# Values of a chunked delta rule: turned in 32x32 blocks by VectorE and placed by four stores, with their row factors moved into the inverse

## The chip, the cores and the metric

The kernel runs on one core of a Trainium2 chip. The metric is the device time of one execution in microseconds (us); the kernel before takes 1234.93 us, the median of three runs (1234.6 to 1235.82).

## The reference

One decoder layer in float32: 1024 tokens, 1024 channels. A shared RMS-norm and input projection feed two groups of heads, differential attention (4 heads) and a gated DeltaNet (4 heads, key and value width 128); both outputs go through one output projection, and a squared-ReLU MLP follows. The change lies in the DeltaNet's delta rule. Cut to what matters:

```python
dn_qkv = causal_conv_silu(dn_qkv, conv_w[l])            # width 4, depthwise
dn_q, dn_k, dn_v = jnp.split(dn_qkv, ...)
dn_q, dn_k = l2_norm(dn_q), l2_norm(dn_k)               # per head of 128
# chunked: k_beta = k * beta, v_beta = v * beta
Lmat = where(strict, einsum('bhncd,bhnjd->bhncj', k_beta, k) * decay, 0)
sol = triangular_solve(Lmat, [v_beta, k_beta * exp(g)], unit_diagonal=True)
u, w = sol[..., :Dv], sol[..., Dv:]
def step(state, inp):                                   # one chunk after the other
    v_new = u_c - w_c @ state
    o = (q_c * exp(g_c)) @ state + qk_c @ v_new
    state = state * exp(g_last) + k_dec.T @ v_new
```

## The kernel before

The kernel uses chunks of 128 tokens, eight in all. The DeltaNet part has two stages.

**Projections and inverse.** `dn_proj(kind)` (L666) projects keys (kind 1), then queries (kind 0), then values (kind 2). Each kind has 4 heads `h` in two halves `hf` of 512 tokens, so 8 groups. A group is 24 products on TensorE (PE) into the PSUM tile `ps_dn` (L265 to L267; two banks), with channels on the partitions and tokens along the row; ScalarE (ACT) copies it to `cp` (L678), and ACT and VectorE (DVE) compute the convolution in `cy` (L680, L682) and SiLU (L690). `skew` hands each group on one group late. Every group is then turned by PE so that tokens lie on the partitions: `transposed(src)` (L713) issues four 128x128 transposes into the PSUM tile `ps_t` (L716). What the second stage needs is parked in DRAM by `park` (L701): `park_d[h, chunk, token, slot, channel]`, one store per group and slot, 512 bytes per token. Slot 0 holds the keys, slot 1 the scaled turned keys, slot 2 the values, slot 3 the queries, slot 4 the masked query-key products.

Keys are not normalised; the factors are carried instead. `vsc` (128 x 32, one column for each head and chunk) holds the square root of the keys' sums of squares `ssk` plus epsilon for each token. The values' turned tile in PSUM is multiplied by `vsc` (L854) into the SBUF tile `kn` (two buffers) and parked in slot 2.

The unit-triangular matrix of each head and chunk (`lt`) is inverted by blocks of 32. The 32x32 diagonal blocks go through DRAM (`fsx_d`, `fsg_d`) and are solved in VectorE by `invert` (L743), which is interleaved with the queries' groups. `horner(hs, hf)` (L797) then builds the inverse W of two heads and one half: 4 loads `gb` a head (L804, rows of 128 bytes), a VectorE block turn (L806), a product `ps_p` (L810) masked into `pb` by VectorE (L813), and three rounds of products `ps_h` (L818; 96, 64 and 32 wide) whose results go back into W, the first by VectorE (L822), the others by ACT (L824). It is called after the values' groups with `hf == 0`, four times: heads 0 and 1, heads 2 and 3 of the first half, then of the second.

**Scan.** `scan` (L902) walks the chunks. It loads slots 0 to 2 of a chunk as `pka` (L910), multiplies the keys with the state, and forms

```python
V.scalar_tensor_tensor(rr_[h], PA[h], neg_eg[:, i:i + 1], pk[:, h, 2, :], ALU.mult, ALU.add)
Wc = W[h, c // 4][:, (c % 4) * P:(c % 4 + 1) * P]
T.matmul(PA[h], Wc, rr_[h], start=True, stop=True)      # contracts over W's rows
```

where `neg_eg` is minus the exponential of the summed gates. For the first chunk `rr_` is slot 2 itself. The product over W sums over the partitions, that is over W's rows and the rows of `rr_`.

**Order.** In the first stage a scheduler orders each engine's instructions by its own simulated times. From the scan on, the class `Interleave` plans the order of PE's work by hand: the scan, the attention's projections (`ps_qk`, L1067 to L1069, with their turns `ps_qkt`, L1028), scores and values of the attention. Nearly all DMAs are issued in order from SyncE's queue (SP): parks, `gb`, the weight quarters `wraw` (L191 and L217), `pka`, `pkb`. A DMA on this queue also waits for the one issued eight before it to land, whose semaphore it takes over.

Of the kernel before, what the change touches and what calls it, by code (L numbers as in the profile page):

```python
# [13 lines left out]
ALU = mybir.AluOpType  # L14
# [106 lines left out]
def tile_hymba_layer(  # L121
# [6 lines left out]
    nc = tc.nc  # L128
    V, S, G, T = nc.vector, nc.scalar, nc.gpsimd, nc.tensor
# [40 lines left out]
    park_d = dram.tile([HEADS, NT, P, 5, P], F32, name="park_d")  # L170
# [212 lines left out]
    def z_raw(tb, u, pool, tag, mid=None, at=2):  # L383

        ps = pool.tile([P, 512], F32, tag=tag, name="ps_z")
        for k in range(KB):
            if k == at and mid is not None:
                z_spread(mid)
            T.matmul(ps[:, :UC], xTs[tb][:, k, :], wz[u][1][k // 2][:, k % 2, :], start=k == 0, stop=k == KB - 1)
        return ps  # L390
# [88 lines left out]
    with tc.manual_schedule(engines={T.engine, V.engine, S.engine, G.engine}):  # L479
# [5 lines left out]
        z = {(0, 0): z_raw(0, 0, pj, "pj")}  # L485
# [43 lines left out]
        for tb in range(3, NT):  # L529
            for u in range(2):  # L530
                nxt, at = spread_at.get((tb, u), (None, 0))
                z[tb, u] = z_mm(tb, u, *pools[tb], nxt, at)
                if nxt is not None:
# [4 lines left out]
                    if nxt in (4, 5):  # L538
                        b = {4: 5, 5: 7}[nxt]
# [32 lines left out]
    ps = ph.tile([P, 512], F32, tag="ph", name="ps_pv")  # L572
# [24 lines left out]
    v4 = lambda t: t.rearrange("p (c d) -> p c d", d=P)  # L597
    c32 = lambda name: sp.tile([P, 32], F32, name=name)
    beta, gg, neg_eg, eg, elast, ediff = (c32(n) for n in ("beta", "gg", "neg_eg", "eg", "elast", "ediff"))
# [35 lines left out]
    ps = ph.tile([P, 512], F32, tag="ph", name="ps_g")  # L635
# [21 lines left out]
    def ta(name, bufs, dt=F32):  # L657
        return sa.tile([P, 512], dt, tag=name, name=name, bufs=bufs)

    ssq, ssk, rq, bp, kds, vsc = smalls + [sp.tile([P, 32], F32, name=n) for n in ("kds", "vsc")]  # L660

    cps = [sa.tile([P, 1028], F32, name=f"cp{i}") for i in range(2)]
    for cp in cps:
# [2 lines left out]
    def dn_proj(kind):  # L666
        for pr in range(2):
            with tc.issue_after(x_last.ins) if kind == 1 and pr == 0 else ExitStack():
                w = load_unit(w_units[6 + 2 * kind + pr])
            for hl in range(2):  # L670
                h = 2 * pr + hl
                u = 4 * kind + h
                cp = cps[hl]
                for hf in range(2):
                    ps = pj.tile([P, 512], F32, tag="pj", name="ps_dn")
                    trn(ps, w, hl * P, hf)
                    b = 512 * hf
                    S.copy(cp[:, 3 + b:3 + b + 512], ps)  # L678
                    y = ta("cy", 2)
                    S.activation(y, cp[:, 3 + b:3 + b + 512], AF.Copy, scale=pv[:, 36 + u:37 + u])  # L680
                    for wi in (2, 1, 0):
                        V.scalar_tensor_tensor(y, cp[:, wi + b:wi + b + 512], pv[:, 12 * wi + u:12 * wi + u + 1],  # L682
                                               y, ALU.mult, ALU.add)
                    if kind == 1:
                        th = ta("cth", 2)
                        S.activation(th, y, AF.Tanh, scale=0.5)
                        yield h, hf, y, th
                    else:
                        o = ta("cth" if hf else "k2", 2)
                        S.activation(o, y, AF.Silu)  # L690
                        yield h, hf, o

    def skew(gen):
        prev = None
        for it in gen:
            if prev is not None:
                yield prev
            prev = it
        yield prev

    def park(h, hf, slot, src):  # L701
        nc.sync.dma_start(park_d[h, 4 * hf:4 * hf + 4, :, slot, :].rearrange("c p d -> p c d"), v4(src))

    def cols4(t, h, hf):
        return t[:, 8 * h + 4 * hf:8 * h + 4 * hf + 4]

    def bc_col(t):
        return t.unsqueeze(2).broadcast_to([P, 4, P])

    def bc_mask(t):  # L710
        return t.unsqueeze(1).broadcast_to([P, 4, P])

    def transposed(src):  # L713
        ps = pt_.tile([P, 512], F32, tag="pt", name="ps_t")
        for c in range(4):
            T.transpose(ps[:, c * P:(c + 1) * P], src[:, c * P:(c + 1) * P], ident)  # L716
        return ps
# [25 lines left out]
    def invert():  # L743

        fxv = fx.rearrange("p (j i) -> p j i", i=32)
        fgv = fg.rearrange("p (r c) -> p r c", c=32)
        nc.sync.dma_start(fx, fsx_d)
        for j in range(31):
            m = 31 - j
            tv = ft[:, :m * (j + 1)].rearrange("p (m c) -> p m c", m=m)  # L750
            V.tensor_tensor(tv, fxv[:, j, j + 1:32].unsqueeze(2).broadcast_to([P, m, j + 1]),
                            fgv[:, j, 0:j + 1].unsqueeze(1).broadcast_to([P, m, j + 1]), ALU.mult)
            V.tensor_tensor(fgv[:, j + 1:32, 0:j + 1], fgv[:, j + 1:32, 0:j + 1], tv, ALU.subtract)
            if j % 8 == 7:
                yield
        nc.sync.dma_start(fsg_d, fg)

    lt = {}
    for h, hf, y, th in skew(dn_proj(1)):
# [3 lines left out]
        ps = transposed(k2)  # L763
# [33 lines left out]
    def horner(hs, hf):  # L797
        pb, z = {}, {}
        for h in hs:
            gb = gbs[h]  # L800
            for b in range(4):
                bs = slice(32 * b, 32 * b + 32)
                p0 = 32 * h + 8 * b + 4 * hf
                nc.sync.dma_start(v4(gb[bs, :])[:, :, bs], fsg_d[p0:p0 + 4, :].rearrange("c (r k) -> r c k", k=32))  # L804
            z[h] = sp.tile([P, 512], F32, tag="lw", name="W", bufs=10)
            V.transpose(z[h], gb)  # L806
        for h in hs:
            ps = ph.tile([P, 512], F32, tag="ph", name="ps_p")
            for c in range(4):
                T.matmul(ps[:, c * P:c * P + 96], lt[h, hf][:, c * P:(c + 1) * P],  # L810
                         gbs[h][:, c * P:c * P + 96], start=True, stop=True)
            pb[h] = sf.tile([P, 512], F32, tag="pb", name="pb", bufs=2)
            V.tensor_tensor(v4(pb[h])[:, :, 0:96], v4(ps)[:, :, 0:96], bc_mask(blk)[:, :, 0:96], ALU.mult)  # L813
        for m in (96, 64, 32):
            for h in hs:
                ps = ph.tile([P, 512], F32, tag="ph", name="ps_h")
                for c in range(4):
                    T.matmul(ps[0:m, c * P:c * P + m], pb[h][:, c * P:c * P + m],  # L818
                             z[h][:, (c + 1) * P - m:(c + 1) * P], start=True, stop=True)
                zv, pv4 = v4(z[h])[0:m, :, P - m:P], v4(ps)[0:m, :, 0:m]  # L820
                if m == 96:
                    V.tensor_tensor(zv, zv, pv4, ALU.subtract)  # L822
                else:
                    S.activation(zv, pv4, AF.Copy, scale=-1.0)  # L824
        for h in hs:
            W[h, hf] = z[h]

    inverse = invert()
    for h, hf, q2 in skew(dn_proj(0)):
        k2 = ta("kr", 2)  # L830
        nc.sync.dma_start(v4(k2), park_d[h, 4 * hf:4 * hf + 4, :, 0, :].rearrange("c p d -> p c d"))
        park(h, hf, 3, q2)
        ps = transposed(q2)
        psm = gram(k2, q2)
        sq = ta("kn", 2)
        for c in range(4):
            i = cidx(h, 4 * hf + c)
            S.activation(sq[:, c * P:(c + 1) * P], ps[:, c * P:(c + 1) * P], AF.Square, accum_out=ssq[:, i:i + 1])
        rstd(cols4(rq, h, hf), cols4(ssq, h, hf), float(P), EPS * P, sp, "rqt", 4)
        qk = ta("qk", 2)  # L840
        for c in range(4):
            i = cidx(h, 4 * hf + c)
            cs = slice(c * P, (c + 1) * P)
            V.scalar_tensor_tensor(qk[:, cs], psm[:, cs], bp[:, i:i + 1], dts[h, hf][:, cs], ALU.mult, ALU.mult)
        park(h, hf, 4, qk)
        next(inverse, None)
# [2 lines left out]

    heads = [((h, h + 1), hf) for hf in range(2) for h in (0, 2)]  # L850
    for h, hf, v2 in skew(dn_proj(2)):
        ps = transposed(v2)
        vs = ta("kn", 2)
        V.tensor_tensor(v4(vs), v4(ps), bc_col(cols4(vsc, h, hf)), ALU.mult)  # L854
        park(h, hf, 2, vs)
        if hf == 0:
            horner(*heads.pop(0))

# [1059 lines left out]
```

## Time and profile before

| | |
|---|---|
| runs, median of 3 (us) | 1234.93 (1234.6 to 1235.82) |
| profiled execution (us) | 1234.74 |
| its span, first to last instruction (us) | 1233.0 |
| granted TensorE clock | 1.000 |
| values' projections and inverse, about (us of the span) | 186 to 253 |
| first product of the scan (us of the span) | 256.56 |
| DMA, mean over the span | 164 GB/s |

The page lists the busy time of each engine (PEld is the loading of weights into PE, which overlaps PE), the chain of work that ended last, the costliest groups of instructions, and the DMA issues. PE's matmuls are pipelined and their ends are modelled, so how much PE loses is read from what it waited for and from the chain rather than from its busy share alone. Rows of the chain give start, length and what; rows of instructions give the number, then the shortest, median and longest duration in ns.

### The profile page before, as it was taken

The numbers are of one execution on the slowest core, as the hardware profiler recorded it, in microseconds if no ns is written. First come the engines' busy times: TensorE is split into PE (matmuls) and PEld (weight loads), VectorE is DVE, ScalarE is ACT, GpSimd is POOL, SyncE is SP. The second block draws the span as 40 slices with busy tenths as digits, with TensorE's granted clock in tenths as the row PEclk, the third lists the DMA queues.
The fourth block names the chain that finished last, engine by engine and source line by source line (L and its number), as shares of the span: only waits on it lengthen the run. The fifth ranks groups of instructions, "written<-read, shape, count | busy, mean of one in ns | idle before, by whom it ended". The sixth has DMA issues, their size and how long they took to land.

```text
span 1233.0 us, 18819 instructions
## 1 busy us (share of the span) xinstructions
PE 1217.3 (99%) x6823; PEld 1054.3 (86%) x6823; DVE 824.7 (67%) x1524; ACT 624.2 (51%) x1249; POOL 151.3 (12%) x215
## 2 busy tenths in 40 slices
PE   9999999999999999999999999999999999999998
PEld 8978888898999998888888888888888888888886
DVE  6868796556647657777799544565569755777543
ACT  6588553344346555566666544444564333333330
POOL 2411110043434421001200000000000000000000
PEclk9999999999999999999999999999999999999999
DMA  9344653278748756323437434444479645423301
GB/s 350 98 115 122 163 162 104 63 234 240 231 148 252 232 162 159 85 77 108 157 117 255 172 122 151 171 170 153 155 241 382 234 179 184 163 103 103 137 35 69
DMA packets 143301, 202.12 MB, mean 164 GB/s; under 512 B 20920, under 2 KB 98280, under 8 KB 143208
## 3 DMA queue, kind: packets, MB, share of 16 engines
q1 hardware_dynamic: 138584, 187.28, 46.9%
q0 software_dynamic: 4480, 13.64, 2.9%
q8 instruction: 54, 0.88, 0.3%
q14 instruction: 39, 0.32, 0.1%
q10 hardware_dynamic: 144, 0.00, 0.0%
HBM read 135.86 MB, written 65.01 MB: 163 GB/s over the span
## 4 chain that ended last, share of the span: by engine, by line
PE 88%; DVE 4%; DMA 3%; ACT 2%; issue 2%; POOL 1%; SPq 1%; POOLq 0%; DVEq 0%; ACTq 0%
PE X L1517 4%; PE X L1515 4%; PE X L1516 4%; PE X L1814 4%; PE X L1815 4%; PE X L1813 4%; PE ps_dn L265 3%; PE ps_dn L267 3%; PE ps_dn L266 3%; PE ps_qk L1067 3%; PE ps_qk L1068 3%; PE ps_qk L1069 3%; PE ps_o L1250 2%; PE Y L1515 2%; PE Y L1517 2%; PE Y L1516 2%
## 5 line engine op out<-in xcount | busy, mean ns | idle before, releaser
L1433 ACT CAST hH<-ur 128x1024 fp32r<-128x1024 f32 x56 | 58.9, 1051 | 173.4 <-PE Y L1814 89.8
L1434 DVE TENSOR_TENSOR hL<-ur,hH 128x1024 fp32r<-128x1024 f32 x56 | 68.3, 1223 | 79.4 <-ACT hH L1433 79.4
L1067 PE MATMUL ps_qk<-wH,hH 128*128 128x256 f32 x384 | 114.3, 298 | 0.0
L1069 PE MATMUL ps_qk<-wH,hL 128*128 128x256 f32 x384 | 108.7, 283 | 0.0
L1068 PE MATMUL ps_qk<-wL,hH 128*128 128x256 f32 x384 | 108.4, 282 | 0.0
L1434 DVE TENSOR_TENSOR op<-raw,op 128x1024 fp32r<-128x1024 f32 x48 | 58.7, 1223 | 74.2 <-PE X L1516 41.1
L1813 PE MATMUL X<-hH 128*128 128x512 f32 x224 | 87.1, 389 | 0.0
L1814 PE MATMUL X<-hL,hH 128*128 128x512 f32 x224 | 87.1, 389 | 0.0
L1815 PE MATMUL X<-hH,hL 128*128 128x512 f32 x224 | 87.1, 389 | 0.0
L265 PE MATMUL ps_dn<-hH,wH 128*128 128x512 f32 x192 | 76.3, 397 | 0.2 <-ACT cp L678 0.2
L267 PE MATMUL ps_dn<-hH,wL 128*128 128x512 f32 x192 | 75.8, 396 | 0.0
L266 PE MATMUL ps_dn<-hL,wH 128*128 128x512 f32 x192 | 75.8, 395 | 0.0
L1068 PEld LDWEIGHTS ps_qk<-wL,hH 128*128 128x128 f32 x384 | 73.4, 191 | 0.2
L1067 PEld LDWEIGHTS ps_qk<-wH,hH 128*128 128x128 f32 x384 | 73.3, 191 | 0.2
L1069 PEld LDWEIGHTS ps_qk<-wH,hL 128*128 128x128 f32 x384 | 73.1, 190 | 0.0
L1434 DVE TENSOR_TENSOR hL<-dw,hH 128x1024 fp32r<-128x1024 f32 x56 | 68.2, 1218 | 0.9 <-ACT hH L1433 0.9
L1433 ACT CAST op<-raw 128x1024 fp32r<-128x1024 f32 x48 | 50.4, 1052 | 35.7 <-PE Y L1517 19.9
L1433 ACT CAST hH<-dw 128x1024 fp32r<-128x1024 f32 x56 | 58.7, 1048 | 10.7 <-DMA dw<-in_w_down_dram 5.0
L1205 ACT ACTIVATE pexp<-pexp,mx 128x128 f32<-128x128 f32 (+7 forms) x64 | 49.7, 777 | 25.1 <-DVE mx L1204 24.5
L682 DVE SCALAR_TENSOR_TENSOR cy<-cp,pv,cy 128x512 f32<-128x512 f32 x72 | 53.7, 747 | 8.1 <-ACT cy L680 7.3
L1340 PE MATMUL ps_op<-wH,hH 128*128 128x512 f32 x128 | 53.0, 414 | 0.0
L1515 PE MATMUL Y<-hH,op 128*128 128x512 f32 x128 | 49.9, 390 | 0.4 <-DVE ua L1555 0.4
(370 smaller groups left out, 3429.1 us busy)
## 6 DMA issues: line engine op xcount, KB each, us to landing
ur<-ud SPq DMA_DIRECT2D x28, 1024.0 KB, 5.0
raw<-in_w_up_dram SPq DMA_DIRECT2D x32, 512.0 KB, 3.9
dw<-in_w_down_dram SPq DMA_DIRECT2D x32, 512.0 KB, 6.8
wraw<-in_w_units_dram SPq DMA_DIRECT2D x48, 256.0 KB, 3.7
qk_d<-qa POOLq DMA_DIRECT2D x32, 256.0 KB, 4.3
ud<-ua SPq DMA_DIRECT2D x16, 512.0 KB, 4.2
ud<-s SPq DMA_DIRECT2D x16, 512.0 KB, 2.7
pka<-park_d SPq DMA_DIRECT2D x32, 192.0 KB, 4.8
```

The costliest lines, as they stand in the source:

```text
L265: T.matmul(ps, lh(k), rh(k), start=(k == 0), stop=False)
L266: T.matmul(ps, lh(k), rl(k), start=False, stop=False)
L267: T.matmul(ps, ll(k), rh(k), start=False, stop=(k == n - 1))
L1067: T.matmul(ps[:, :256], hH[:, k, sl], wh[:, k, :], start=(k == 0), stop=False)
L1068: T.matmul(ps[:, :256], hH[:, k, sl], wl[:, k, :], start=False, stop=False)
L1069: T.matmul(ps[:, :256], hL[:, k, sl], wh[:, k, :], start=False, stop=(k == KB - 1))
L1433: S.copy(dst[0], src)
L1434: V.tensor_tensor(dst[1], src, dst[0].bitcast(F32), ALU.subtract)
L1515: T.matmul(ps, op[0][:, k, cs], h[0][:, k, :], start=start and k == 0, stop=False, skip_group_check=True)
L1813: T.matmul(bank[t], v[0][:, j, sl], v[2][:, j], start=s0, stop=False, skip_group_check=True)
L1814: T.matmul(bank[t], v[0][:, j, sl], v[3][:, j], start=False, stop=False, skip_group_check=True)
L1815: T.matmul(bank[t], v[1][:, j, sl], v[2][:, j], start=False, stop=s1, skip_group_check=True)
```

## The change

The values' groups are no longer turned on PE. VectorE's transpose turns each 32x32 block of the 128x512 tile in place, from SBUF to SBUF, so that inside a block tokens lie on the partitions, while the blocks stay where channels were on the partitions. Four stores for each group then put the blocks where they belong in slot 2: store `a` takes the 32 partitions of channel block `a` and writes, for each of its 512 tokens, 32 channels (128 bytes). The values are parked without the factor `vsc`. The factor is multiplied into W instead: after `horner` has finished a head, VectorE multiplies W's rows by `vsc`. Since the other term of `rr_` would then get the factor too, `neg_eg` is divided by `vsc` once, ahead of the queries' groups; the tile for the reciprocals, `rvs`, is that of `ssk`, which is not read any more.

```diff
     ssq, ssk, rq, bp, kds, vsc = smalls + [sp.tile([P, 32], F32, name=n) for n in ("kds", "vsc")]
+    rvs = ssk
...
+    def put_blocks(dst, src):
+
+        for a in range(4):
+            s = slice(32 * a, 32 * a + 32)
+            nc.sync.dma_start(dst[:, s].rearrange("(b s) r -> s b r", s=32),
+                              src[s].rearrange("s (b r) -> s b r", r=32))
...
         for h in hs:
+            V.tensor_tensor(v4(z[h]), v4(z[h]), bc_col(cols4(vsc, h, hf)), ALU.mult)
             W[h, hf] = z[h]
 
+    V.reciprocal(rvs, vsc)
+    V.tensor_tensor(neg_eg, neg_eg, rvs, ALU.mult)
     inverse = invert()
...
     for h, hf, v2 in skew(dn_proj(2)):
-        ps = transposed(v2)
         vs = ta("kn", 2)
-        V.tensor_tensor(v4(vs), v4(ps), bc_col(cols4(vsc, h, hf)), ALU.mult)
-        park(h, hf, 2, vs)
+        V.transpose(vs, v2)
+        put_blocks(park_d[h, 4 * hf:4 * hf + 4, :, 2, :].rearrange("c p d -> (c p) d"), vs)
         if hf == 0:
             horner(*heads.pop(0))
```

## The prediction

> **What bounds the kernel now.** I read the page first, then PE's own waits over the whole span, then the stretches around the change, then the chain through them.
>
> ```profile
> span 1233.0 us, 18819 instructions
> PE 1217.3 (99%) x6823; PEld 1054.3 (86%) x6823; DVE 824.7 (67%) x1524; ACT 624.2 (51%) x1249; POOL 151.3 (12%) x215
> PE 88%; DVE 4%; DMA 3%; ACT 2%; issue 2%; POOL 1%; SPq 1%; POOLq 0%; DVEq 0%; ACTq 0%
> PE ps_qkt L1028 <- DVE qn L1092: 1.3, 2, 1.0
> PE ps_dn L265 <- ACT cp L678: 0.2, 1, 0.2
> ```
>
> PE is busy 99% of the span and carries 88% of the chain; the longest waits it has on another engine in mid-kernel are near 1 us, and in the projections that the change touches (ps_dn) there is one of 0.2 us. So an instruction taken from PE's queue is worth its place there, as long as nothing else becomes late. Next, the stage: up to 186 us the keys and queries are projected, 186 to 231 are the projections of the values with the first two pairs of heads of the inverse, 231 to 257 the rest of the inverse up to the scan's first product (columns: start and end, length, PE, PEld, DVE, ACT, POOL busy, granted clock, DMA share, GB/s).
>
> ```profile
> 130.00:186.00 56.00, 56.00 (x300) 47.61 (x299) 51.04 (x138) 30.43 (x99) 8.16 (x8) 1.00 0.59 164
> 186.00:231.00 45.00, 45.00 (x273) 38.09 (x272) 28.89 (x53) 15.50 (x34) 1.01 (x1) 1.00 0.33 88
> 231.00:240.00 9.00, 9.00 (x93) 8.59 (x92) 4.31 (x7) 4.19 (x10) 0.00 (x0) 1.00 0.30 90
> 240.00:257.00 17.00, 16.40 (x177) 15.42 (x176) 8.76 (x22) 4.72 (x15) 3.81 (x4) 1.00 0.42 132
> ```
>
> PE is full until 240. VectorE is busy 28.89 + 4.31 + 8.76 = 41.96 of 71 us (59%), the DMA engines a third. Only behind 240 does PE stand idle at times: there the small products of the inverse wait for VectorE and ScalarE. The chain through the stage (start, length, what; longest pieces):
>
> ```profile
> 189.29 0.44 PE ps_t L716 x4
> 196.79 0.44 PE ps_t L716 x4
> 200.88 0.44 PE ps_t L716 x4
> 211.34 0.59 PE ps_t L716 x4
> 216.22 0.59 PE ps_t L716 x4
> 220.71 1.76 PE ps_p L810 x16
> 223.88 0.44 PE ps_t L716 x4
> 226.17 1.36 PE ps_h L818 x16
> 231.55 1.08 PE ps_h L818 x16
> 232.63 0.59 PE ps_t L716 x4
> 235.73 0.62 PE ps_h L818 x16
> 236.35 0.32 PE ps_qk L1067
> 238.94 0.88 PE ps_p L810 x8
> 240.94 0.52 DVE pb L813
> 242.07 0.58 DVE kn L854
> 253.26 0.26 PE ps_qkt L1028
> 256.72 0.34 PE ps_A L930 x3
> ```
>
> **The change part by part.** *PE's turns go.* Eight groups of four transposes leave the queue. Seven of them stand in the chain: 4 x 0.44 + 3 x 0.59 = 3.53 us; the eighth, in the idle stretch behind 240, I take at 0.44. Sum 3.97, 4.0 us. The lower bound is 8 x 0.44 = 3.5: the three longer ones follow a ps_h and may hold some of its end, which another product would then pay.
>
> *VectorE.* Eight products from PSUM (L854) go, eight block turns of the same 128x512 come, eight products over W, and two small 128x32 operations. The trace has both kinds:
>
> ```profile
> L854 DVE TENSOR_TENSOR kn<-ps_t,vsc x8: 650/683/692, 190.1 to 242.0; 128x512 f32<-128x512 f32 x8
> L806 DVE STREAM_TRANSPOSE W<-gb x8: 690/702/712, 196.8 to 241.4; 128x512 f32<-128x512 f32 x8
> L822 DVE TENSOR_TENSOR W<-W,ps_h x8: 532/544/551, 205.6 to 251.1; 96x384 f32<-96x384 f32 x8
> ```
>
> The turn costs 0.702 for 0.683, no difference. The product over W does not occur before; its row neighbours are L854 (0.683 for 512 columns) and L822 (0.544 for 384, in proportion 0.73). I take 0.68: 8 x 0.68 = 5.4 us, VectorE at 47.4 of 71 us (67%). In the sum over the stage that is free, PE's work hides it; in VectorE's queue it is not, see the tail. The turn no longer waits for PE, which makes it due earlier, as soon as ScalarE's SiLU has written the values. The scaled neg_eg is made while the queries are projected (the first of the three stretches, where VectorE is 51.04 of 56 us busy) and read in the scan; two operations of 32 columns are under 0.68 each by the rows for 512, and PE is full there all the same: nothing.
>
> *The stores.* Each 256 KB store of 512 runs of 512 B becomes four of 64 KB with 512 runs of 128 B. Thirty-two instead of eight on SP's queue, ahead of the small gb loads of the inverse (L804), the weight loads (L191, L217) and, at the end, the scan's pka loads.
>
> ```profile
> L702 SPq DMA_DIRECT2D park_d<-kn x8: 370/378/642, 190.8 to 242.7; - x8
> DMA to landing us min/median/max: 2.3/2.3/2.3
> 200.63 3.38 SPq L804 DMA_DIRECT2D gb<-fsg_d  x7
> gb<-fsg_d SPq DMA_DIRECT2D x32, 16.0 KB, 1.9
> fsx_d<-lt SPq DMA_DIRECT2D x32, 16.0 KB, 1.7
> q1 hardware_dynamic: 1010, 0.12, 24.1%
> q1 hardware_dynamic: 525, 0.26, 81.6%
> 249.42 3.66 SPq L910 DMA_DIRECT2D pka<-park_d  x8
> pka<-park_d SPq DMA_DIRECT2D x32, 192.0 KB, 4.8
> SPq L702 <- DVE kn L854: 13.1, 5, 8.0
> ```
>
> The two q1 rows are the queue between 196.8 and 200 us (gb loads alone, 128 B runs) and between 226 and 227 (one store alone, 512 B runs): 0.241 x 16 x 3.2 / 1010 = 12 ns of a DMA engine per short run, 0.816 x 16 x 1.0 / 525 = 25 ns per long one. So 32 x 512 = 16384 short runs cost 16384 x 12 ns / 16 = 12.5 us of all engines, where 8 x 512 x 25 / 16 = 6.5 went before: 6 us more in 71 at a share of a third. On SP an issue costs 0.378 whatever the run size, if it goes by the number of runs (512 in both): 24 x 0.378 = 9.1 us more on a queue that stands 13.1 us waiting for kn alone (last row). The other bound is that it goes by short runs as the gb loads do: 3.38 / 7 = 0.48 us for 128 of them, so 1.93 for 512. I take 0.38, since the store row has the very count of runs and only their size differs. Who waits behind the stores: gb (needed for ps_p; in the built order the first ps_p stands 63 projection products behind the last query product where it stood 48 behind, so loads late by 3 x 0.378 = 1.1 us find a later reader), the last two weight quarters L191 (ScalarE's cast waits for them with the next PSUM copies behind it; ps_dn's second bank gives it one group of projections), and pka.
>
> *The tail, where the cover goes.* The built order moves 24 ps_qk products to before the second pair's last ps_h; behind it stand 18 instead of 42, all of them in pair three. PE's work from that ps_h's end (236.35) to the first ps_qkt (253.26): 42 ps_qk at (238.94 - 236.35) / 20 = 0.13, 5.5 us; two pairs at 1.76 + 1.36 + 1.08 + 0.62 = 4.82, 9.6; one ps_t, 0.44. That is 15.5 of 16.9 us, so 1.4 idle. After: 18 x 0.13 + 9.6 = 12.0 and the idle time worked out by VectorE's order. Pair three: its pb products stand behind two products over W (2 x 0.68, from 0.3 us after the last ps_h of pair two), then pb 0.52, turn 0.70, pb 0.52: the second pb ends 3.4 us in, PE has had 1.76 + 0.68 = 2.4 us of work: 0.9 idle. Pair four: W, half as wide a qn product, W (0.68 + 0.34 + 0.68) ahead of pb, 0.5 idle against ps_p. The hops from ps_h over VectorE or ScalarE to the next ps_h cost the idle 1.4 of before in four of them, 0.35 each; three stand uncovered now, 1.05. Sum 2.4, 1.0 more than before, although the kn product of 0.58 leaves that chain; bounds 1.4 (nothing more) and twice the 2.4. The first pb of pair four also gates pka (it holds the memory that the scan's tiles take): it issues at 249.42, 7.3 us ahead of the scan's first product (256.72), and would now by the same working stand some 6.5 ahead; four of the eight loads are out in half of 3.66 us and land in 4.8 (median of all): 6.6, just enough.
>
> **Sum.** 1234.74 (profiled execution: span 1233.0 and 1.74 around it) - 4.0 + 1.0 = 1231.7; the median of the runs, 1234.93, lies 0.19 above the profiled one, so 1231.9 us. All after the scan's start keeps its order on PE and only starts earlier.
>
> **The rivals.** *The tail eats it* (about the same as before). VectorE's queue is in order and W's products wait for ScalarE; if the unshown product costs more, or hops meet badly, the idle 2.4 doubles or the scan waits for pka besides: 1.5 to 3.3 more, 1233.4 to 1235.2. For it: 0.6 us of PE idle in the last row of stretches already. Against: only two pairs are uncovered.
>
> *SP's queue becomes the bound* (slower). If a store holds SP 1.93 us, 32 take 61.8, the gb loads 32 x 0.48 = 15.4, six weight loads at a store's 0.38 2.3: 79.5 us, where the queue has 63.4 (186 to the pka issue at 249.42). The scan would start 16.1 us late: 1251. It decides from (63.4 - 4 - 17.7) / 32 = 1.3 us a store. Against it: 0.378 for as many runs, and fsx_d, short runs into DRAM too, landing in 1.7 us. The Trainium skill, page "DMA: Bandwidth & Descriptors", section Specifications, names 512 B as the smallest transfer for line rate and says that below it the engines read, modify and write; by that each short run would cost twice, an estimate of 25 us of all engines in place of 12.5, which still fits the free two thirds and would only push toward this rival. The trace's 12 ns a short run does not show it.
>
> *The turns were not worth their place*: PE loses 4 us of work but the next wait takes it all (weight casts, pkb loads in the scan). 1234.9. It lies within the first rival's band, and shares its chance.
>
> **How the numbers follow.** Two runs can be told apart at about 0.2%, 2.5 us: faster means under 1232.5, slower over 1237.4. Forecast 0.62, of which 0.54 under 1232.5 and 0.08 the same; better still (part of the old idle 1.4 goes too, 1234.9 - 4.0 - 1.4 = 1229.5 at the most) 0.06; tail or next wait 0.22, of it 0.20 the same and 0.02 slower; SP's queue 0.10, slower. Faster 0.60, same 0.28, slower 0.12. The range goes from the best case, 1229.5, to the end of the tail rival, 1235.2; SP's queue is left out.
>
> **What would show it.** Right: no ps_t for the values; PE without waits till the second pair; the first ps_qkt near 250.3 and the scan's first product near 253.7 in place of 253.26 and 256.7; stores at 0.4 us on SP, landing near 2.3. Wrong: stores over 1 us on SP, ps_dn waiting for cp or ps_p for gb; PE idle over 3 us between 236 and 253; scan products waiting for pka; or a gain at 253 that later waits take back.

## The result and the profile after

| | before | changed |
|---|---|---|
| runs side by side, median of 20 each (us) | 1235.93 (1234.24 to 1238.19) | 1233.68 (1231.83 to 1236.04) |
| profiled execution: span (us) | 1233.0 | 1231.8 |
| profiled execution: mean granted clock | 1.000 | 0.998 |

The ratio is 0.9986, 95% interval [0.9979, 0.9992]: about 1.7 us faster (1.0 to 2.6), where 3.0 were forecast. (The medians of the table lie 2.25 apart, inside that interval.) The change does gain, but by the prediction's own bar of 0.2% (faster means under 1232.5 us) it falls under "the same", to which it gave 0.28; "faster" had 0.60. The absolute forecast was 1231.9.

The page of the changed kernel shows PE as full as before, with 32 matmuls fewer:

```profile
span 1231.8 us, 18793 instructions
PE 1215.3 (99%) x6791; PEld 1052.0 (85%) x6791; DVE 829.9 (67%) x1534; ACT 624.3 (51%) x1249; POOL 151.3 (12%) x215
PE 90%; DMA 3%; DVE 2%; ACT 2%; issue 1%; SPq 1%; POOL 1%; DVEq 0%; ACTq 0%; POOLq 0%
```

The four stretches of the stage (columns as in the prediction):

```profile
130.00:186.00 56.00, 56.00 (x302) 47.75 (x301) 51.78 (x140) 30.87 (x104) 8.15 (x8) 1.00 0.58 164
186.00:231.00 45.00, 45.00 (x272) 38.43 (x271) 32.62 (x59) 17.57 (x35) 1.01 (x1) 1.00 0.49 95
231.00:240.00 9.00, 8.69 (x88) 7.71 (x87) 5.72 (x12) 2.86 (x9) 0.00 (x0) 1.00 0.39 86
240.00:257.00 17.00, 16.76 (x174) 15.67 (x174) 9.68 (x25) 6.11 (x16) 4.62 (x6) 1.00 0.49 157
```

VectorE is at 48.0 of 71 us (forecast 47.4), and the DMA engines rise from 0.33 to 0.49 between 186 and 231. The new operations, by line:

```profile
L709 SPq DMA_DIRECT2D park_d<-kn x32: 302/494/552, 185.5 to 235.6; - x32
DMA to landing us min/median/max: 1.8/2.0/3.7
L864 DVE STREAM_TRANSPOSE kn<-k x4: 670/707/711, 184.8 to 224.4; 128x512 f32<-128x512 f32 x4
L864 DVE STREAM_TRANSPOSE kn<-cth x4: 670/709/717, 191.1 to 233.4; 128x512 f32<-128x512 f32 x4
L834 DVE TENSOR_TENSOR W<-W,vsc x8: 676/684/693, 220.1 to 250.9; 128x512 f32<-128x512 f32 x8
```

A turn takes 0.708 us and a product over W 0.684, as taken. A store holds SP 0.494 us instead of 0.378, and lands in 2.0. The chain through the tail:

```profile
235.69 0.28 ACT W L832
235.99 1.25 DVE W L834 x2
237.25 0.51 DVE pb L821
238.87 0.92 PE ps_h L826 x8
245.15 0.60 DVE W L834
250.09 0.26 PE ps_qkt L1038
253.56 0.89 PE ps_A L940 x8
```

The scan's first product is at 253.56 in the chain, 3.16 us earlier than before (256.72), and yet the span is only 1.2 us shorter. In the chain behind it stands one thing that was smaller before: a wait for `pkb`, the scan's load of the queries and the masked query-key products, at the fourth chunk. Among the waits of PE between 250 and 320 us, before (with one more that matters below) and after:

```profile
PE ps_o L970 <- DMA pkb<-park_d: 1.2, 1, 1.2
PE ps_qkt L1028 <- ACT qn L1086: 0.8, 1, 0.8
```

```profile
PE ps_o L980 <- DMA pkb<-park_d: 2.8, 1, 2.8
```

PE's start times aligned instruction by instruction show it: the changed kernel is 3.16 us ahead up to 298 us, 1.6 ahead at that product and 0.4 ahead 2.3 us later. At the next product it is 1.3 ahead again, because there the kernel before waits 0.8 us for ScalarE (second row above) and the changed one does not. From 315 to 360 us it is 0.35 ahead, and from 700 us to the end 1.16.

### The profile page after: what moved, and what is told of

It is laid out like the page before. It is cut to its first block, busy times and chain, and to the rows that moved or that the text cites. A ratio compares the mean times of both kernels' runs of the same rounds, so it can differ in the third digit from the quotient of the medians.

```text
span 1231.8 us, 18793 instructions
## 1 busy us (share of the span) xinstructions
PE 1215.3 (99%) x6791; PEld 1052.0 (85%) x6791; DVE 829.9 (67%) x1534; ACT 624.3 (51%) x1249; POOL 151.3 (12%) x215
## 4 chain that ended last, share of the span: by engine, by line
PE 90%; DMA 3%; DVE 2%; ACT 2%; issue 1%; SPq 1%; POOL 1%; DVEq 0%; ACTq 0%; POOLq 0%
PE X L1527 5%; PE X L1526 5%; PE X L1525 5%; PE X L1825 4%; PE X L1823 4%; PE X L1824 4%; PE ps_dn L265 3%; PE ps_dn L267 3%; PE ps_dn L266 3%; PE ps_qk L1077 3%; PE ps_qk L1079 3%; PE ps_qk L1078 3%; PE Y L1525 3%; PE Y L1526 3%; PE Y L1527 3%; PE ps_o L1260 2%
## 5 line engine op out<-in xcount | busy, mean ns | idle before, releaser
L1352 PE MATMUL ps_op<-wH,hL 128*128 128x512 f32 x128 | 50.3, 393 | 0.0
```

## Two yardsticks

One profile of each kernel is not enough here: where the stage begins varies by up to 1.4 us from execution to execution, from causes ahead of the change. So I split each profile in two: the **stage**, from the last group of query-key products (`ps_m`) to the scan's first product, and the **rest**, from there to the end of the span. The rows (start, length, instruction), first of before, then of the changed kernel:

```profile
185.69 1.06 PE L723 MATMUL ps_m<-cth,kr 128*128 128x128 f32 x8
256.56 1.06 PE L930 MATMUL ps_A<-pka,W 128*128 128x128 f32 x8
```

```profile
185.10 1.06 PE L731 MATMUL ps_m<-cth,kr 128*128 128x128 f32 x8
253.40 1.06 PE L940 MATMUL ps_A<-pka,W 128*128 128x128 f32 x8
```

The stage takes 70.87 us before and 68.30 after: 2.57 us gained. The other 0.59 of the 3.16 was a lead that this execution had already at 185 us, so 0.57 of the 1.16 at the end is the change's. (Expectations below that name 70.09 and 67.50 count from the last product of the same group, 0.78 us later.) All runs by these yardsticks:

| kernel | stage | rest | ratio of the runs to before |
|---|---|---|---|
| before | 70.87 | 976.4 | 1 |
| changed | 68.30 | 978.4 | 0.9986 [0.9979, 0.9992] |
| e1 before, early load | 70.87 | 980.1 | 1.0014 [1.0005, 1.0023] |
| e2 changed, early load | 68.28 | 979.6 | 0.9989 [0.9980, 0.9998] |
| e3 turn only | 68.14 | 979.0 | 0.9990 [0.9980, 1.0000] |
| e4 fill at the second chunk | 68.28 | 981.4 | 0.9998 [0.9988, 1.0009] |
| e5 before, KS later | 70.87 | 976.7 | 0.9984 [0.9975, 0.9993] |
| e6 changed, KS later | 68.29 | 976.4 | 0.9973 [0.9962, 0.9984] |
| e7 same, W deferred | 68.15 | 976.4 | 0.9976 [0.9967, 0.9985] |
| e8 changed, fill at the fourth chunk | 68.29 | 976.2 | 0.9974 [0.9963, 0.9984] |
| e9 as e5 | 70.86 | 976.1 | 0.9988 [0.9980, 0.9997] |
| e10 as e6 | 68.27 | 975.7 | 0.9970 [0.9959, 0.9981] |
| e11 stores twice | 77.05 | 978.6 | 1.0067 [1.0054, 1.0081] |
| e12 factors only | 70.87 | 976.7 | 0.9994 [0.9986, 1.0003] |

Stage and rest are from one profile of each run, the ratio from all executions. The stage repeats to 0.03 us wherever its code is the same; the rest does not.

## The experiments

My theory: the stage gains what the change takes from PE less a dearer tail, and at the scan's fourth chunk a load that is not there as much sooner takes part of it back. Rivals: the tail or the stores cost more than seen; the loss behind 298 us is chance.

**The give-back.** In the changed kernel, 1 MB of `KS` (the attention's keys, four loads) is issued right ahead of the fourth chunk's `pkb`. It is first used 75 us later, by the scores at 362 us.

```profile
286.84 2.71 SPq L1128 DMA_DIRECT2D KS<-qk_d  x4
289.66 2.11 SPq L970 DMA_DIRECT2D pkb<-park_d  x4
```

*First try, at the wrong chunk.* e1 and e2 fetch part of the second chunk's data sooner, with four `pkb` buffers instead of five to make room:

```diff
+            if c == 0:
+                for h in range(HEADS):
+                    pq1[h] = sb.tile([P, P], F32, tag="pq", name="pq", bufs=4)
+                    nc.sync.dma_start(pq1[h], park_d[h, 1, :, 3, :])
...
-            pkb[h] = sb.tile([P, 2, P], F32, tag="pkb", name="pkb", bufs=5)
-            nc.sync.dma_start(pkb[h], park_d[h, c, :, 3:5, :])
+            pkb[h] = sb.tile([P, 2, P], F32, tag="pkb", name="pkb", bufs=4)
+            ...    # slot 4 alone for c == 1; ps_o reads pq1 there
```

> The kernel before, with one load of the scan issued sooner: the query halves of the second chunk (four tiles, 64 KB each) go to SP's queue right behind the second chunk's pka instead of behind the loads of KS; the other halves stay where they were. Theory (the gain is given back at the scan's first product fed by pkb): the 1.2 us that PE waits there before goes, 0 to 1.2 us faster than before, ratio 0.9990 to 1.0000. Rival (later waits of another kind set the time): no change, 1.0000.

> The changed kernel with the same load issued sooner. Theory: the wait of 2.8 us at the first ps_o goes, and with it the four microseconds at a granted clock near 0.5; PE stays 2.5 to 3.1 us ahead of before from 250 past 300 us, and the run ends 2.5 to 4 us sooner than before, ratio 0.9968 to 0.9980. Rival (the next wait takes it whatever is done here, or DMA landing times do): ratio 0.9986 as without the edit, the offset falling back to 1 us by 315.

Neither came out: I had miscounted the chunks. The wait at 298 us is the fourth chunk's, so the early load hid nothing; with one buffer less, all four of that chunk's `pkb` loads instead of three stand behind KS. The kernel before became 1.7 us slower (1.0014), with waits of 2.7 us in three pieces in place of 1.2 in one. The changed one kept its 2.7 us. So the buffers and the queue there matter to both kernels.

*e4 and e8, a fill.* Twelve extra products ahead of `ps_o`, overwritten by the real ones, at the second chunk (e4, the same miscount) and at the fourth (e8):

```diff
             o1 = pB.tile([P, 512], F32, tag="pB", name="ps_o1")
+            if c == 1:                # e8: c == 3
+                for r in range(12):
+                    T.matmul(o1[:, (r % 4) * P:(r % 4 + 1) * P], ident, Sold[r % 4], start=True, stop=True)
```

> The changed kernel with twelve extra 128x128 products ahead of the scan's first ps_o, written into the bank that the real products overwrite: 2.5 us of idle PE work in the place where PE stands idle for 3 us. Theory (the granted clock falls because PE stood idle): the clock stays at 0.9 or more from 297 to 302 us, ps_qk products there take 0.12 us again instead of 0.21, and the run ends 0.5 to 1.5 us sooner than the changed kernel, ratio to before 0.9976 to 0.9982. Rival (the clock falls for another cause, or the slow stretch is made up later): ratio 0.9986 or, by the work added, up to 0.9996.

> The changed kernel with KS where it was and twelve extra 128x128 products, 2.6 us, ahead of the fourth chunk's ps_o, in the place where PE stands idle for 3 us (the fill of e4 stood one idle stretch too early, at 272). Theory (the clock falls because PE stood idle, and that costs by itself): the real ps_o products still start at about 297 with the loads, the clock stays at 0.95 or more from 297 to 302, the run ends 0.5 to 1.5 us sooner than the changed kernel, ratio to before 0.9974 to 0.9983. Rival (the slow stretch is made up by later slack): 0.9984 to 0.9990.

e4 put 2.7 us of work where PE was busy, at 272 us. By the runs that costs about 1.5 us (0.9998 against 0.9986), by its one profile 3.0. But as PE came 2.7 us later to the fourth chunk, it waited there only 1.5 us at a stretch, and the clock stayed at 1.00. e8 put the same work into the idle time, and the kernel became faster, 0.9974; that interval overlaps the one without the fill, but in the profiles the rest is 2.2 us shorter. The stretches 293 to 297 and 297 to 302 us, of before, of the changed kernel and of e8:

```profile
293.00:297.00 4.00, 4.00 (x37) 4.00 (x36) 2.19 (x8) 2.85 (x11) 1.24 (x2) 1.00 1.12 247
297.00:302.00 5.00, 2.97 (x22) 2.50 (x21) 3.30 (x12) 0.80 (x3) 1.56 (x3) 1.00 1.05 331
```

```profile
293.00:297.00 4.00, 1.19 (x12) 1.00 (x10) 1.61 (x7) 0.00 (x0) 2.14 (x3) 1.00 1.11 298
297.00:302.00 5.00, 5.00 (x28) 4.88 (x29) 2.38 (x7) 1.08 (x3) 0.60 (x1) 0.66 0.60 200
```

```profile
293.00:297.00 4.00, 4.00 (x38) 4.00 (x37) 2.97 (x12) 0.85 (x4) 2.56 (x3) 1.00 1.13 292
297.00:302.00 5.00, 5.00 (x46) 5.00 (x45) 2.60 (x7) 1.65 (x5) 0.98 (x2) 1.00 0.80 276
```

The changed kernel does 28 matmuls in the five microseconds behind its idle 2.8 us, at a granted clock of 0.66 on average; e8, which was not idle, does 46 at 1.00. The chain of the changed kernel has it product by product, 0.21 us in place of 0.12:

```profile
282.91 3.86 DMA qk_d<-qa
286.84 0.69 SPq L1128
289.66 7.24 DMA pkb<-park_d
296.94 1.35 PE ps_o L980 x6
298.29 0.21 PE ps_qk L1077
```

The clock alone, one microsecond of it (299 to 300; the one before and the one behind it are alike):

```profile
299.00:300.00 1.00, 1.00 (x6) 1.00 (x6) 1.00 (x6) 0.00 (x0) 0.00 (x0) 0.50 0.44 144
```

So the loss there is the wait and, on top, a slow clock that the wait sets off: e8 has PE wait for the same load, with the gap filled, and keeps 1.00. The slow clock took 1.2 us of PE's lead (1.6 to 0.4); 0.9 of it came back at once, at the product for which the kernel before waits. The Trainium skill, page "TensorE: Matmul & The Clock Gate", Part 1, describes such a gate: half rate after an idle window of about 3.4 us. The half rate agrees (0.50 from 298 to 301 us); the gap that set it off here was shorter, 2.8 us.

*e5 and e6, the cause taken away.* KS's loads go behind the fifth chunk's `pkb` on SP's queue; PE's and VectorE's orders stay as they are.

```diff
+        with tc.issue_after(newest["pkb"].ins):    # the last pkb load of c == 4
-        heads[0] = load_head(0, ap), load_v(0, ap)
+            heads[0] = load_head(0, ap), load_v(0, ap)
```

> The kernel before, with the four loads of KS (256 KB each, first used at 362 us) issued on SP's queue behind the loads of pkb of the fifth chunk instead of ahead of those of the fourth. Theory (PE waits for the fourth chunk's pkb because KS's 1 MB stands ahead of it): the wait of 1.2 us at the fourth chunk's ps_o goes, ratio 0.9988 to 0.9998. Rival (pkb lands late whatever stands ahead of it): 1.0000.

> The changed kernel with the loads of KS issued behind the fifth chunk's pkb. Theory: the wait of 2.8 us goes, the granted clock stays at 1.00 from 297 to 302 us, PE stays about 3.2 us ahead of before past 300 us, and the run ends 2.7 to 3.7 us sooner than before, ratio 0.9970 to 0.9979. Rival (the gain is taken by whatever wait comes next in the scan): PE falls back to 1 us ahead by 315, ratio 0.9984 to 0.9990.

In e6 the fourth chunk's loads land sooner (first row below; 6.6/6.7/6.8 in the changed kernel), `ps_o` does not wait for them there, the clock is 1.00, and the run is 3.3 us faster than before, as the theory has it. (Its profile has a shorter wait for `pkb`, 1.3 us, two chunks on; that of e10 has 0.2.)

```profile
DMA to landing us min/median/max: 4.2/4.3/4.3
290.40 1.83 SPq L970 DMA_DIRECT2D pkb<-park_d  x4
305.33 0.64 SPq L1130 DMA_DIRECT2D KS<-qk_d  x1
297.00:302.00 5.00, 3.96 (x36) 3.79 (x34) 4.08 (x13) 2.32 (x5) 2.23 (x4) 1.00 0.69 234
```

But e5 gained more than expected, 2.0 us. Its wait at the fourth chunk is gone too, as the loads land in 3.2 us instead of 5.4. Where all of the 2.0 lies is not shown: in its profile PE is 1.7 us ahead of before's at 299 us, counted from the scan's first product, and has lost that again by 700 us. Nor is KS the whole difference between the two kernels: with it out of the way the changed kernel's loads still land 1.1 us later (4.3 against 3.2), with it in front 1.3 later (6.7 against 5.4). In e4, the changed kernel with KS issued at 290.68 us instead of 286.84, they took 5.3, as before; so it is not the new stores that make them slow, but what they meet at that time, which was not traced further.

Measured by the pair e5 and e6, the change is worth 1.8 us, hardly more than without the edit. That called for a second pair:

> The kernel before with KS's loads moved (the kernel of e5) once more, as partner of the next run, on the same chip. Read so far: from the last product of the queries to the scan's first product the kernels before take 70.09 us in each of three profiles, the changed ones 67.50 in each of five. Theory (all of those 2.6 us lasts to the end once KS stands behind): this kernel's mean lies 2.2 to 3.0 us above that of the next. Rival (later waits still take a part): 1.0 to 2.0 us.

> The changed kernel with KS's loads moved (the kernel of e6) once more. Theory: ratio to before 0.9964 to 0.9975, and in no run a mean clock of 0.998 or less, where the changed kernel without that edit has one in about half of its runs; stage from the queries' last product to the scan's first 67.5 us. Rival: 0.9976 or more.

The forecast for e10 came out (0.9970, no mean clock of 0.998 or less). The means of the pairs' runs differ by 1.77 (1233.74 and 1231.97) and by 2.21 us (1233.49 and 1231.28), the second just inside what the theory named; all 22 against all 13 runs give 1.97, plus or minus 0.55. It falls on the border between theory and rival: by that interval more than half of the stage's 2.57 is there, and all of it just misses. In the profiles of e5, e6, e9 and e10 the rest is 976.7, 976.4, 976.1 and 975.7 us, so these four show no loss of the changed kernel against its partner behind the scan's start once KS is out of the way.

**The tail.** e3 leaves the factors out, e7 keeps them and takes the last four products over W out of the tail:

```diff
e3
-            V.tensor_tensor(v4(z[h]), v4(z[h]), bc_col(cols4(vsc, h, hf)), ALU.mult)
-    V.reciprocal(rvs, vsc)
-    V.tensor_tensor(neg_eg, neg_eg, rvs, ALU.mult)
e7 (on top of e6)
-            V.tensor_tensor(v4(z[h]), ...)
+            if hf == 0:
+                V.tensor_tensor(v4(z[h]), ...)
...                                   # in the scan, chunks 0 to 3, behind the last head's new state
+                        with tc.issue_after(sn_.ins):
+                            V.tensor_tensor(v4(W[c, 1]), v4(W[c, 1]), bc_col(cols4(vsc, c, 1)), ALU.mult)
```

> The changed kernel without the row factors: the eight products over W, the reciprocal and the scaling of neg_eg are left out, so the values enter unscaled and the result is not the reference's. It prices the tail by itself. Theory: without products over W in VectorE's queue the tail keeps its old idle time, the first ps_qkt comes 4.0 us sooner than before instead of 3.2, at 249.3; at the scan's first ps_o it waits for the same loads, so the end gains little of that: ratio 0.9980 to 0.9988. Rival (the tail is free): 250.1 as with the factors.

> As the run before it, and besides the four products over W of the last two pairs of heads, which the scan reads first in its fifth chunk, are taken out of VectorE's queue in the tail and put behind the scan's first four updates of the state. Theory: the first ps_qkt comes 4.0 us sooner than before instead of 3.2, as without any factors, and with KS out of the way that lasts: ratio 0.9962 to 0.9974. Rival (0.7 us more of VectorE's work in each of the scan's first chunks lies on the scan's chain): no better than the run before it, 0.9970 to 0.9984.

The rivals were right in both (e7's interval alone would not tell, the stage does): without the products in the tail the stage is 68.14 and 68.15 us, 0.15 shorter, not 0.8, and e7 is no faster than e6. e12 does the opposite, the factors without the turn:

```diff
     ps = transposed(v2)
     vs = ta("kn", 2)
-    V.tensor_tensor(v4(vs), v4(ps), bc_col(cols4(vsc, h, hf)), ALU.mult)
+    V.tensor_copy(vs, ps)
     park(h, hf, 2, vs)                # and the products over W, rvs, neg_eg as in the change
```

> The kernel before with the row factors alone: TensorE turns the values and one store per group parks them, as before, but VectorE copies them unscaled, and the products over W, the reciprocal and the scaling of neg_eg are there. It prices the factors without the turn. Theory (leaving the factors out of the changed kernel took only 0.15 us off the stage): the stage takes 70.1 to 70.4 us against 70.09, ratio 0.9996 to 1.0006. Rival (each product over W in the tail is paid, 0.7 us a pair): 71 us or more, ratio over 1.0006.

The stage takes 70.87 us as before, the time is unchanged. Moving the factors is free in the kernel before and costs 0.15 us of the stage in the changed one (e3, e7); the whole gain, and nearly the whole price of the tail, belong to the turns.

**The stores.** e11 issues each one twice.

```diff
         put_blocks(park_d[h, 4 * hf:4 * hf + 4, :, 2, :].rearrange("c p d -> (c p) d"), vs)
+        put_blocks(park_d[h, 4 * hf:4 * hf + 4, :, 2, :].rearrange("c p d -> (c p) d"), vs)
```

> The changed kernel with each of the 32 block stores issued twice (the same data to the same place). It prices the stores. Theory (they lie in SP's free time): 32 more at 0.49 us are 16 us more on SP in 66 us, and the stage still takes 67.5 us; ratio to before 0.9982 to 0.9992. Rival (SP's queue is near its limit, or short runs load the DMA engines): the stage takes over 68.5 us, ratio over 0.9994.

Here the rival was right, and by much: the stage grows by 8.75 us. SP's queue carries the last weight quarters (L191) behind the stores. They are issued at 207.08 us before, at 213.87 in the changed kernel, and at 238.12 and 243.57 in e11:

```profile
207.08 0.85 SPq L191 DMA_DIRECT2D wraw<-in_w_units_dram  x2
```

```profile
213.87 0.94 SPq L191 DMA_DIRECT2D wraw<-in_w_units_dram  x2
```

```profile
238.12 0.38 SPq L191 DMA_DIRECT2D wraw<-in_w_units_dram  x1
243.57 0.49 SPq L191 DMA_DIRECT2D wraw<-in_w_units_dram  x1
PE ps_qk L1078 <- ACT wH L192: 6.5, 2, 6.3
```

PE waits 6.3 us for ScalarE's cast of them, and its clock is 0.50 in the end of that wait and behind it, from 238 to 247 us, so a part of the 8.75 us is slow clock. Nor is all of the delay the 32 added stores' own time (32 x 0.49 = 15.7 us): the scheduler put the weight loads behind more of the blocks, so that 56 stores stand ahead of the first of them where 20 stood (36 x 0.49 = 17.6 us of the 24 that it is later), and SP waits 1.1 us for stores to land. So e11 bounds the reserve rather than pricing one store: the queue that was 7 us late without harm cannot be 30 us late.

## Why the prediction was right and wrong

*PE's turns: right in kind, 4.0 was too much.* Start to start over the whole stage, PE's time goes as follows (us, before and after): `ps_t` 3.01 and 0; `ps_dn` 34.67 and 34.03; `ps_p` and `ps_h` 20.43 and 21.46; `ps_qk` and `ps_qkt` 11.94 and 12.00. A turn costs its own place and a slower product behind it:

```profile
189.13 0.60 PE L716 MATMUL ps_t<-ident,k 128*128 128x128 f32 x4
189.49 0.47 PE L265 MATMUL ps_dn<-hH,wH 128*128 128x512 f32 x1
189.80 0.39 PE L266 MATMUL ps_dn<-hL,wH 128*128 128x512 f32 x1
190.02 0.39 PE L267 MATMUL ps_dn<-hH,wL 128*128 128x512 f32 x1
```

0.36 for the turn and 0.31 instead of 0.23 for the next product, 0.44 in all. Eight of these are 3.5, and 3.01 + 0.64 = 3.65 were gained. The sum's 4.0 took the three rows of 0.59 in full; those held some of a `ps_h`'s end, which the prediction named as its lower bound.

*The tail: 1.0 came out by luck.* `ps_p` and `ps_h` take 1.03 us more. The prediction reached 1.0 with 0.9 and 0.5 us of idle time behind the products over W in VectorE's queue and 1.05 in the hops, less the 1.4 of before. But by e3 and e7 the products over W are worth only 0.15 of the stage, although the chain runs through them (`W L834` above): without them something else ends almost as late. The rest, 0.9, fits the uncovered hops between the inverse's small products (three at 0.35 in the prediction), with the `ps_qk` products moved ahead of them; that split was argued and not tried, since PE's order is the scheduler's.

*Stage: 3.0 forecast, 2.57 gained.* 3.65 less 1.03 less 0.06. Also as forecast: no `ps_t` for the values, no wait of PE over 0.2 us in the stage, neither `pka` nor `gb` late.

*The step that failed is the last one: "All after the scan's start keeps its order on PE and only starts earlier."* The order was kept; the start was not all that counted. (With 1.0 to 2.6 us measured by the runs, the stage's 2.57 is only just within the interval; that something is lost behind it rests on the profiles and on the edits of KS and the fill.) The prediction's own sign of that, "a gain at 253 that later waits take back", came true. The waits of a whole span had been read and 1.2 us for `pkb` was no more than "near 1 us"; what was not asked is whether this load comes as much sooner as PE does. KS waits for a `qk_d` store and its landing, `pkb` stands behind KS's 1 MB, and in the changed kernel it took 7.24 us to land (the chain above), where before the chain had:

```profile
286.07 3.48 DMA qk_d<-qa
289.62 0.68 SPq L1118
292.43 6.03 DMA pkb<-park_d
298.51 1.18 PE ps_o L970 x6
```

The issues did move with PE: the `qk_d` store went out 3.16 us sooner (282.91 for 286.07 us). But it took 3.86 us to land instead of 3.48, so KS and `pkb` were issued only 2.8 us sooner, and `pkb` landed 1.2 us more slowly, so the product that needs it came only 1.6 sooner. A gap of 1.2 us became one of 2.8, long enough for the clock to fall.

How often it falls is known only roughly. Mean clocks of 0.998 or less were seen in 8 of 20 runs of the changed kernel and in 6 of 82 of the kernel before; with KS later or the gap filled (e5 to e10) in none of 53. The changed kernel was not run side by side with those; but among runs that were side by side, e2 and e3, which keep the gap, have 14 of 22 and e4, which shortens it, none of 11. A mean of 0.999 decides nothing: a fall of 3.4 us alone leaves 0.9986, and the end of the span, where PE has no work left, counts too (0.50 from 1230 to 1231 us in the changed kernel). Runs of the changed kernel at 1.000 have a mean of 1233.0, those at 0.998 or less 1234.6, and the four at 0.999 are as slow, 1234.8. An estimate from the 8 runs alone: 1.6 us in four runs of ten, 0.6 on average, against about 0.1 before, with the longer wait included. That would be about half of the 0.9 between 2.57 and the measured 1.7.

*What stays open.* Even with KS later the runs show 1.97 +- 0.55 of 2.57. Whether the remaining 0.6 is lost somewhere behind the scan, or is the spread of 13 and 22 runs, these runs do not decide. Nor do they show why the store and `pkb` took longer to land.

*SP's queue as the bound: not so, but nearer than 0.10 and "from 1.3 us a store" suggest.* A store took 0.494, between the 0.378 taken and the 1.93 of the bound. Yet the working looked at `pka` at the queue's end; e11 shows that the first to be late are the weight quarters in its middle, and there twice the stores, about 1 us of SP where one took 0.494, are already too much, though part of that delay is the changed order. The Trainium skill, page "DMA: Bandwidth & Descriptors", section Specifications, has transfers under 512 B read, modified and written. The DMA share rose by 0.16 of 45 us and 0.09 of 9 between 186 and 240, 8.0 us of all engines; with the 6.5 that went, an estimate for the 16384 short runs is 14.5 us, so 14 ns each, near the prediction's 12 and not twice that. The trace does not show the rule's price.

*The number.* The gain of 3.0 us was forecast against 1.7 measured, and 1231.9 us against 1233.68. 1231.9 used a baseline of 1234.93, the median of three runs; with 20 to 33 runs the kernel before had medians of 1234.94 to 1235.93. The range, 1229.5 to 1235.2, held.

## What to carry to other kernels

A microsecond gained on the busiest engine is kept only as far as the next load that does not move with it: for each wait of that engine behind the change, small ones too, ask what issues the load, what stands ahead of it on its queue, and whether it lands as much sooner. A large transfer that is needed late should not stand ahead of a small one that is needed now: moving KS back was worth 1.5 to 2.0 us by itself, and both together 3.3 to 3.7 us (0.9973 and 0.9970), the fastest version here. And where executions differ by more than the effect, split the profile at two instructions around the change: the stage repeated to 0.03 us while whole runs varied by 4.

## What the runs showed of the hardware

A short idle gap of PE can lower its clock. After 2.8 us without work (and 2.7 in e2 and e3, 3.1 in e11) the granted clock was 0.50 for three to four microseconds, and in e1 it fell so after a gap of 1.7; gaps of 1.2 (before) and 1.5 us (e4) left it at 1.00. In the changed kernel the fall cost 1.2 us of PE's lead on top of a wait that had grown by 1.6, and 2.7 us of useless products in the gap made the kernel about 1.5 us faster.

Stores of 128-byte runs landed in 2.0 us, sooner than those of 512-byte runs (2.3), each with 512 runs; it was SP, at 0.494 instead of 0.378 us an issue and four times as many, that paid for them.
